# A hybrid decoder block on one core: which queue the third pair of experts' weights and the left-over rows come by, and when the place table is worked out

## The chip, the cores and the metric

The kernel runs on one core of a Trainium2 chip. The metric is the device time of one execution in microseconds (us), the median over several executions. A core has a matrix engine (TensorE, PE in the profile), two vector engines (VectorE, DVE, and ScalarE, ACT), GpSimd (POOL) and SyncE (SP). Transfers between the main memory and the on-chip memory are asked for by a queue of one of these engines. In this kernel SP's queue asks for nearly all weights, POOL's for everything that is gathered or scattered by row numbers.

## The reference

One decoder block over 512 tokens of width 1024: a state-space branch and a latent attention branch, a cross-attention to a memory, and a mixture of experts with 32 experts, of which each token takes two out of one group of eight. The change is in the mixture of experts alone:

```python
def hierarchical_moe(h, w_rg, b_rg, w_re, b_re, w_gate, w_up, w_down):
    ...
    g_sel = jnp.argmax(g_logits, axis=-1)
    ...
    top_v, top_i = lax.top_k(e_in, TOP_K)
    w_top = jax.nn.softmax(top_v, axis=-1) * g_w
    ...
    hg = jnp.einsum('td,edf->tef', t, w_gate)
    hu = jnp.einsum('td,edf->tef', t, w_up)
    act = jax.nn.silu(hg) * hu * combine[:, :, None]
    y = jnp.einsum('tef,efd->td', act, w_down)
    return y.reshape(b, s, d)
```

All data are float32. An expert's three matrices (gate and up 1024 x 256, down 256 x 1024) are 1024 KB each.

## The kernel before

The stages ahead of the experts and the routing, which finds every token's two experts, fill about the first 930 us of the profiled execution. The expert stage works on 16 *pairs* of experts, numbered 0 to 15 (`pr` in the code, `NP = 16`). Each expert has 64 places, so that a pair fills 128 rows, and places of which there are fewer tokens stay empty. (Tokens beyond 64 of an expert are handled after the loop; nothing there is touched.)

A pass of the loop over pairs does, for its pair `pr`:

- `gate_up(pr)`: 32 products of the gathered rows with the gate and up weights; after them it asks for the gate and up weights of pair `pr + 3` (`load_gate_up`, four transfers of 1024 KB). There are six slots for such weights (`gslots`), two to a pair, so three pairs are held.
- `hidden(pr)`: ACT and DVE form the hidden values (tile `ea`).
- `dispatch(pr + 1)`: eight transposes of the next pair's rows and their scaling on DVE into `XG`.
- `down_rows(pr - 1)`: the pair before's down product (`py`), and what becomes of it. It then asks for the down weights of pair `pr + 2` (`load_down`, two transfers; their tile is `dn`, or `dw` for every third pair).
- `turn(pr)`: two transposes of the hidden values for the down product of the next pass.
- `places(c)` in every second pass: the place table `PI[c]` for the two pairs of `c`, eight small products (`pinf`), one copy and 15 operations of DVE on 128 x 2 elements. It holds which token each place has, its weight and its scale. `onehots(c)` in the passes between builds the one-hot matrices for it.
- `fetch(pr + 3)`: POOL gathers that pair's rows (`GRt<-tD`) by the place table; an empty place's row number is out of bounds and skipped. There are two row buffers, `GR[0]` and `GR[1]`.

What becomes of a pair's down product differs. Pairs 0 to 6 (`NS = 7`): the 128 rows are scattered by POOL to a buffer in main memory (`yD<-YB`), at the place of their token. Pairs 7 to 15: the rows are added to the residual `h` at once, by products with one-hot matrices (`pcm`) and eight additions of DVE (`add_rows`). The rows that went to main memory are read back in 16 pieces of 256 KB (`left_rows`, tile `Yt<-yD`, two buffers), two at a time, the first two at the end of pass 7; in each of the passes 8 to 15, `add_left(2)` adds the two pieces that were asked for one pass earlier (DVE, `h<-h,Yt`) and then asks for the next two. Before, POOL's queue asks for them. These passes from 8 on are called *late* in the code.

Every engine and every queue takes its instructions in the order in which this stage's code gives them (`tc.manual_schedule()`). A transfer into a slot waits until the last reader of the slot is done. Besides, the transfers of SP and ACT use eight completion semaphores in turn, and one that is issued waits until the transfer that used its semaphore before has landed, eight transfers earlier. So about eight are under way at most.

Before the loop, `first_rows(0)` and `first_rows(1)` find the token numbers of the first two pairs by a product of one-hot matrices with the token numbers (`ptk`) and gather their rows by these; an empty place asks for row 0. `keep_warm(n)` is n transposes of the identity (`pw`) that nothing reads.

Of the kernel before, what the change touches and what calls it, by code (L numbers as in the profile page):

```python
# [11 lines left out]
I32 = mybir.dt.int32  # L12
# [5 lines left out]
S, D, M = 512, 1024, 256  # L18
NT, KD = S // 128, D // 128
# [10 lines left out]
def block(tc, nc, I, out, dbg=None):  # L30
# [3 lines left out]
    V, A, G, T = nc.vector, nc.scalar, nc.gpsimd, nc.tensor  # L34
# [7 lines left out]
    def pA(name="pa"):  # L42
        return ps.tile([128, 512], F32, name=name, tag="A", bufs=4)
# [29 lines left out]
    def keep_warm(n, p=None):  # L73

        p = pB("pw") if p is None else p
        for _ in range(n):
            T.transpose(p[:, :128], ident, ident)
# [145 lines left out]
    ss = const([128, NT], name="ss")  # L223
# [36 lines left out]
    p = pA()  # L260
# [707 lines left out]
    def gslot(pr, s, shape, name):  # L968
        return sb.tile(shape, F32, name=name, tag=gslots[(2 * pr + s) % 6])

    def load_gate_up(pr, ss=(0, 1)):
        for s in ss:
            w = gslot(pr, s, [128, 2, KD, 256], "gu")
            for j, m in enumerate(("w_exp_gate", "w_exp_up")):
                nc.sync.dma_start(w[:, j], I[m][0, pr * 2 + s].rearrange("(p k) n -> p k n", p=128))
            WG.setdefault(pr, []).append(w)

    def load_down(pr):
        tag = dslots[pr % 3]
        if tag:  # L980
            w = sb.tile([128, 2, 2, D], F32, name="dn", tag=tag)
            w = [w[:, s] for s in range(2)]
        else:
            w = [sb.tile([128, 2, D], F32, name="dw", tag="wr", bufs=2) for _ in range(2)]
        for s in range(2):
            nc.sync.dma_start(w[s], I["w_exp_down"][0, pr * 2 + s].rearrange("(p k) n -> p k n", p=128))
        WD[pr] = w


# [115 lines left out]
    def onehots(c):  # L1105

        for t in range(NT):
            o = OHs[c == 1][:, t]
            V.tensor_scalar(o, iot1[:, :256], slc[:, c - 1, 0, t:t + 1], None, op0=OP.is_equal)
            stt(o, iot1[:, :256], slc[:, c - 1, 1, t:t + 1], f(o), OP.is_equal, OP.add)  # L1110
# [8 lines left out]

    chain = ExitStack()  # L1120
    chain.enter_context(tc.manual_schedule())
    load_gate_up(2)
    load_down(2)
    for t in range(0, NT, 2):
        q = slice(t, t + 2)
        vn = sb.tile([128, 2], F32, name="vn", tag="rsv", bufs=4)
# [100 lines left out]
    def gather(pr, ix, **k):  # L1227
        G.indirect_dma_start(out=GR[pr % 2], out_offset=None, in_=tD, in_offset=bass.IndirectOffsetOnAxis(ap=ix, axis=0), **k)  # L1228

    def first_rows(j):  # L1230

        p = pB("ptk")
        ix = ov[:, 300 + j:301 + j].bitcast(I32)
        for t in range(NT):
            T.matmul(p[:, :2], OHs[0][:, t, j * 128:(j + 1) * 128], tok2[:, t], start=t == 0, stop=t == NT - 1)
        V.tensor_scalar(ix, p[:, :1], -1.0, 0.0, op0=OP.add, op1=OP.max)  # L1236
        gather(j, ix)

    def dispatch(pr):

# [7 lines left out]

    def places(c):

        p = pA("pinf")
        for j in range(2):
            for t in range(NT):
                T.matmul(p[:, j * 8:j * 8 + 8], OHs[c == 1][:, t, j * 128:(j + 1) * 128], info[:, t],
                         start=t == 0, stop=t == NT - 1)
        pi = PI[c] = ov[:, 216 + c % 3 * 26:242 + c % 3 * 26]
        V.tensor_copy(pi[:, :16], p[:, :16])
        col = lambda i: pi[:, :16].rearrange("p (j x) -> p x j", x=8)[:, i]
        ix, sx = (ov[:, o + c % 3 * 2:o + 2 + c % 3 * 2].bitcast(I32) for o in (300, 306))
        u, wa, w, hr, r = (pi[:, 16 + 2 * i:18 + 2 * i] for i in range(5))  # L1260
        V.tensor_scalar(u, col(0), 0.0, 4096.0, op0=OP.is_equal, op1=OP.mult)
        V.tensor_add(u, u, col(0))
        V.tensor_scalar(ix, u, -1.0, None, op0=OP.add)
        V.tensor_add(r, col(6), col(7))
        V.tensor_scalar(hr, r, 0.5, None, op0=OP.mult)
        V.tensor_sub(w, col(5), hcol)
        V.tensor_scalar(w, w, 4.0 * c, None, op0=OP.is_equal)
        stt(u, w, -float(S), u, OP.mult, OP.add)
        V.tensor_scalar(sx, u, S - 1.0, None, op0=OP.add)
        V.tensor_add(wa, col(1), col(2))  # L1270
        V.tensor_mul(w, w, wa)
        V.tensor_add(wa, col(3), col(4))
        V.tensor_add(w, w, wa)
        V.tensor_mul(r, r, r)
        V.tensor_mul(w, w, r)

    def fetch(pr):

        gather(pr, ov[:, 300 + pr // 2 % 3 * 2 + pr % 2:301 + pr // 2 % 3 * 2 + pr % 2].bitcast(I32),
               bounds_check=S - 1, oob_is_err=False)  # L1280
# [86 lines left out]
    first_rows(0)  # L1367
    first_onehots(1)
    first_rows(1)
    gfin = fo = None  # L1370
    wcol = lambda pr: PI[pr // 2][:, 20 + pr % 2:21 + pr % 2]
    hcol_ = lambda pr: PI[pr // 2][:, 22 + pr % 2:23 + pr % 2]
# [19 lines left out]
    def add_rows(pr, after=None):  # L1392
        combine(oTs.pop(pr), 128, after)
# [3 lines left out]
    def left_rows(n):  # L1397

        for i in range(ny[0], min(ny[0] + n, 16)):
            s, t, c = i // 8, i // 2 % 4, i % 2  # L1400
            G.dma_start(Yt[0][:, c], yD[s * S + t * 128:s * S + (t + 1) * 128, c * 512:(c + 1) * 512])
            ny[0] += 1

    def add_left(n):
# [4 lines left out]
            ny[1] += 1  # L1409
        left_rows(n)  # L1410

    keep_warm(6)
    dispatch(0)
    keep_warm(8)
    for pr in range(NP):
        p = gate_up(pr)
        if pr == 0:
            weights()
            onehots(1)
            dispatch(1)  # L1420
            places(1)
            fetch(2)
            fetch(3)
            places(0)
        HG[pr] = hidden(p, 128, "ea", hcol_(pr))
        if pr == 0:
            onehots(2)
            continue
        if pr == 1:
            turn(0)  # L1430
        late = pr > NS
        if late:
            down_rows(pr - 1)
        if pr + 1 < NP:
            dispatch(pr + 1)
        c = pr // 2 + 2
        if pr % 2 and c < NP // 2:
            places(c)
        elif c < NP // 2 and not late:
            onehots(c)  # L1440
        if pr + 3 < NP:
            fetch(pr + 3)
        if not late:
            down_rows(pr - 1)
        turn(pr)
        if pr == 2:
            overflow()
        if late:
            add_rows(pr - 1)
            add_left(2)  # L1450
            if pr % 2 == 0 and c < NP // 2:
                onehots(c)
        if pr == NS:
            Yt.append(sb.tile([128, 2, 512], F32, name="Yt", tag="WL0"))
            left_rows(2)
            W2.append([sb.tile([128, 512], F32R, name=f"Wx{i}", tag=t) for i, t in enumerate(("acT", "selP"))])
            W2.append([x[:, i * 512:(i + 1) * 512] for x in [sb.tile([128, 1024], F32R, name="Wy", tag="WL2")] for i in range(2)])
        if pr == NP - 2:
            fo = gslot(NP - 3, 0, [128, NT, D], "fo")
            gfin = gslot(NP - 3, 1, [128, D], "gfin")  # L1460
            row_bcast(gfin, I["norm_final"], D)
# [104 lines left out]
```

## Time and profile before

| | before |
|---|---|
| device time, median of 3 runs | 1220.15 us (1219.07 to 1221.02) |
| profiled execution: device time | 1216.74 us |
| profiled execution: span, first to last instruction | 1215.0 us |
| PE busy in the span | 1165.5 us (96%) |
| DVE / ACT / POOL busy | 732.1 / 498.0 / 95.2 us |
| moved by DMA in the span | 209.22 MB, mean 172 GB/s |

The profiled execution is 3.4 us shorter than the median of the runs, and 1.74 us of it lie outside the span. The page cuts the span in 40 slices of 30.4 us: in the last ten or so the DMA engines are busy nine tenths and more, at 416 to 421 GB/s. PE's busy time counts matmuls whose ends are modelled, so it is no measure of its speed.

### The profile page before, as it was taken

To read this page: it belongs to the slowest core of one execution; us is meant where nothing else is said; L and a number is where in the kernel's file an instruction comes from. 1 tells how busy PE (TensorE), PEld (TensorE's weight loads), DVE (VectorE), ACT (ScalarE), POOL (GpSimd) and SP (SyncE) were. 2 spreads that over 40 slices of the span, in tenths; PEclk is the share of its full clock that TensorE was granted. 3 is DMA by queue.
4 is the path that set the end of the run, shared out by engine and by line. 5 is a ranking of instruction groups with operands and counts; after the bars stand their busy time and mean duration, and the time that the engine had idled before them with its cause. 6 is when DMAs were issued, how large, how long until landed. Compare 5 with 4: busy or idle time off the path is not lost. (4 is left out here: it accounts for less than half of the span.)

```text
span 1215.0 us, 15732 instructions
## 1 busy us (share of the span) xinstructions
PE 1165.5 (96%) x5930; PEld 846.5 (70%) x5930; DVE 732.1 (60%) x1490; ACT 498.0 (41%) x941; POOL 95.2 (8%) x118
## 2 busy tenths in 40 slices
PE   8999999999999999999999999999997999999992
PEld 7786777777888888887776888988886433434441
DVE  4387788778872334646776745744525744467654
ACT  5434856767443123447775424533421011101112
POOL 0101112111000000101110000000000011111001
PEclk9999999999999999999999999999998899999996
DMA  3532424432323234320225373562817699999961
GB/s 114 160 113 63 144 67 137 122 115 62 97 94 104 70 104 123 98 60 22 55 83 178 105 242 104 174 214 70 339 42 312 248 417 421 416 417 417 417 279 70
DMA packets 103755, 209.22 MB, mean 172 GB/s; under 512 B 13343, under 2 KB 71484, under 8 KB 91390
## 3 DMA queue, kind: packets, MB, share of 16 engines
q1 hardware_dynamic: 96782, 193.11, 44.1%
q0 software_dynamic: 6320, 12.99, 3.2%
q10 hardware_dynamic: 576, 2.10, 0.4%
q8 instruction: 47, 0.77, 0.3%
q14 instruction: 30, 0.25, 0.1%
HBM read 199.33 MB, written 12.12 MB: 174 GB/s over the span
## 5 line engine op out<-in xcount | busy, mean ns | idle before, releaser
L150 DVE TENSOR_TENSOR WLt<-wr,WHt 128x1024 fp32r<-128x1024 f32 x124 | 153.4, 1239 | 176.4 <-ACT WHt L149 99.0
L149 ACT ACTIVATE WHt<-wr 128x1024 fp32r<-128x1024 f32 x125 | 132.2, 1059 | 267.9 <-PE pa L126 158.9
L126 PE MATMUL pa<-uh,WHt 128*128 128x512 f32 x488 | 128.0, 399 | 2.4 <-ACT WHt L149 2.4
L126 PE MATMUL pa<-ul,WHt 128*128 128x512 f32 x488 | 126.2, 397 | 0.0
L126 PE MATMUL pa<-uh,WLt 128*128 128x512 f32 x488 | 125.1, 394 | 0.0
L1296 PE MATMUL pgu<-gu,GRt 128*64 128x512 f32 x512 | 116.1, 598 | 0.9 <-DMA gu<-in_w_exp_up_dram 0.9
L126 PEld LDWEIGHTS pa<-uh,WHt 128*128 128x128 f32 x488 | 89.8, 188 | 23.1 <-ACT WHt L149 2.8
L126 PEld LDWEIGHTS pa<-ul,WHt 128*128 128x128 f32 x488 | 91.3, 190 | 19.2 <-issue 0.7
L126 PEld LDWEIGHTS pa<-uh,WLt 128*128 128x128 f32 x488 | 90.8, 188 | 19.6 <-issue 1.2
L1296 PEld LDWEIGHTS pgu<-gu,GRt 128*64 128x64 f32 x512 | 36.2, 138 | 70.6 <-issue 67.9
L1285 ACT ACTIVATE ea<-pgu,ov 128x256 f32<-128x256 f32 x16 | 7.6, 473 | 146.8 <-PE pgu L1296 133.9
L55 DVE SCALAR_TENSOR_TENSOR ea<-ea,pgu 128x256 f32<-128x256 f32 x16 | 6.7, 421 | 79.4 <-ACT ea L1285 79.4
L711 DVE TENSOR_REDUCE sm<-psc 128x1 f32<-128x512 f32 (+2 forms) x64 | 30.4, 489 | 23.5 <-PE psc L709 20.3
L1339 DVE TENSOR_TENSOR h<-h,pcm 128x512 f32<-128x512 f32 x72 | 43.8, 679 | 0.0
L1316 PE MATMUL py<-dn,aT 128*64 128x512 f32 x176 | 42.5, 617 | 0.0
L712 ACT ACTIVATE Pq<-psc,sm 128x512 f32<-128x512 f32 (+2 forms) x64 | 33.2, 528 | 10.6 <-DVE sm L711 10.2
L1228 POOL DMA_INDIRECT GRt<-tD,ov x16 | 16.5, 1030 | 260.8 <-DVE ov L1236 142.6
L55 DVE SCALAR_TENSOR_TENSOR y<-pa,cols,y 128x509 f32<-128x509 f32 (+2 forms) x48 | 34.7, 744 | 1.6 <-ACT y L383 1.4
L126 PE MATMUL pa<-yl,WHt 128*128 128x512 f32 x128 | 32.8, 396 | 0.0
L126 PE MATMUL pa<-yh,WLt 128*128 128x512 f32 x128 | 32.3, 394 | 0.0
L126 PE MATMUL pa<-yh,WHt 128*128 128x512 f32 x128 | 32.2, 393 | 0.0
L459 ACT ACTIVATE dc<-S6t,ac 128x128 f32<-128x128 f32 x96 | 30.4, 388 | 0.8 <-POOL y L476 0.8
(513 smaller groups left out, 2263.1 us busy)
## 6 DMA issues: line engine op xcount, KB each, us to landing
gu<-in_w_exp_gate_dram SPq DMA_DIRECT2D x32, 1024.0 KB, 19.8
gu<-in_w_exp_up_dram SPq DMA_DIRECT2D x32, 1024.0 KB, 21.7
wr<-in_w_in_dram SPq DMA_DIRECT2D x26, 1024.0 KB, 5.5
dn<-in_w_exp_down_dram SPq DMA_DIRECT2D x22, 1024.0 KB, 22.2
dw<-in_w_exp_down_dram SPq DMA_DIRECT2D x10, 1024.0 KB, 21.2
wr<-in_w_ssd_out_dram SPq DMA_DIRECT2D x8, 1024.0 KB, 5.0
wr<-in_w_xkv_dram SPq DMA_DIRECT2D x8, 1024.0 KB, 5.0
S6t<-ac_d SPq DMA_DIRECT2D x24, 256.0 KB, 4.2
```

The source lines that it names most:

```text
L55: V.scalar_tensor_tensor(o, a, s, b, op0=op0, op1=op1, **k)
L126: T.matmul(o, a(k)[x], b(k)[y], start=first and n == 0, stop=last and n == 3 * nk - 1)
L149: A.activation(h, raw, AF.Copy)
L150: lo.tensor_tensor(l, raw, f(h), op=OP.subtract)
L459: A.activation(dc[:, cs], R[:, cs], AF.Relu, scale=-1.0, bias=ac[:, c * 32 + h:c * 32 + h + 1])
L711: V.reduce_max(mx, dst, axis=AX.X, negate=True)
L712: A.activation(P[:, ROFF[qc]:ROFF[qc] + n], dst, AF.Exp, bias=mx, accum_out=sm[:, 1, s, qc:qc + 1])
L1228: G.indirect_dma_start(out=GR[pr % 2], out_offset=None, in_=tD, in_offset=bass.IndirectOffsetOnAxis(ap=ix, axis=0), **k)
L1285: A.activation(a[:, :256], p[:n, :256], AF.Tanh, scale=hr)
L1296: T.matmul(p[s * 64:(s + 1) * 64].rearrange("p (j n) -> p j n", j=2), XG[:, k, s * 64:(s + 1) * 64], gu[s][:, :, k], start=k == 0, stop=k ...
L1316: T.matmul(p[s * 64:(s + 1) * 64], aT[:, k, s * 64:(s + 1) * 64], dn[s][:, k, hf * 512:(hf + 1) * 512], start=k == 0, stop=k == 1)
L1339: V.tensor_add(h[:, t, hs], h[:, t, hs], p)
```

## The change

It has five parts.

1. The loads of pair 2, six transfers, all stood on SP's queue ahead of everything in this stage. Now the four that fill the pair's second expert's gate and up slot and both down slots stand on POOL's queue: gate and up behind the gathers of pairs 0 and 1, down behind the gather of pair 2.
2. `first_rows` now serves pairs 2 and 3 as well, in place of `fetch(2)` and `fetch(3)`. `onehots(1)` moves ahead of the first `dispatch`, and the place tables 0 and 1 are made in that order.
3. The 6 and 8 transposes of `keep_warm` around the first `dispatch` become 14 ahead of it.
4. In the late passes, `places(c)` is split: its products and the copy stay where they were, its 15 small operations and the gather of pair `pr + 3` follow the eight additions of `add_rows`.
5. The pieces `Yt` are asked for by SP's queue and no longer by POOL's.

```diff
-    def load_gate_up(pr, ss=(0, 1)):
+    def load_gate_up(pr, ss=(0, 1), q=nc.sync):
...
-                nc.sync.dma_start(w[:, j], I[m][0, pr * 2 + s].rearrange("(p k) n -> p k n", p=128))
+                q.dma_start(w[:, j], I[m][0, pr * 2 + s].rearrange("(p k) n -> p k n", p=128))
...
-    load_gate_up(2)
-    load_down(2)
+    load_gate_up(2, (0,))
...
-    def first_rows(j):
+    def first_rows(pr):
 
         p = pB("ptk")
-        ix = ov[:, 300 + j:301 + j].bitcast(I32)
+        ix = ov[:, 300 + pr:301 + pr].bitcast(I32)
+        j = pr % 2
         for t in range(NT):
-            T.matmul(p[:, :2], OHs[0][:, t, j * 128:(j + 1) * 128], tok2[:, t], start=t == 0, stop=t == NT - 1)
+            T.matmul(p[:, :2], OHs[pr // 2][:, t, j * 128:(j + 1) * 128], tok2[:, t], start=t == 0, stop=t == NT - 1)
         V.tensor_scalar(ix, p[:, :1], -1.0, 0.0, op0=OP.add, op1=OP.max)
-        gather(j, ix)
+        gather(pr, ix)
...
     first_rows(1)
+    load_gate_up(2, (1,), G)
+    onehots(1)
...
-            G.dma_start(Yt[0][:, c], yD[s * S + t * 128:s * S + (t + 1) * 128, c * 512:(c + 1) * 512])
+            nc.sync.dma_start(Yt[0][:, c], yD[s * S + t * 128:s * S + (t + 1) * 128, c * 512:(c + 1) * 512])
...
-    keep_warm(6)
+    keep_warm(14)
     dispatch(0)
-    keep_warm(8)
+    first_rows(2)
+    load_down(2, G)
     for pr in range(NP):
         p = gate_up(pr)
         if pr == 0:
             weights()
-            onehots(1)
             dispatch(1)
-            places(1)
-            fetch(2)
-            fetch(3)
-            places(0)
+            first_rows(3)
+            run(places(0))
+            run(places(1))
...
-        if pr % 2 and c < NP // 2:
-            places(c)
-        elif c < NP // 2 and not late:
-            onehots(c)
-        if pr + 3 < NP:
-            fetch(pr + 3)
-        if not late:
+        places_c = places(c) if pr % 2 and c < NP // 2 else iter(())
+        if late:
+            next(places_c, None)
+        else:
+            run(places_c)
+            if pr + 3 < NP:
+                fetch(pr + 3)
+            if pr % 2 == 0:
+                onehots(c)
             down_rows(pr - 1)
...
         if late:
             add_rows(pr - 1)
+            run(places_c)
+            if pr + 3 < NP:
+                fetch(pr + 3)
             add_left(2)
```

Three places of the instruction order show it. The first is SP's queue at the end of the routing, where the loads of pair 2 and then those of pair 3 stand (a `gu` row is one gate or up matrix, `-` is before, `+` is now):

```order
 L975 DMA gu<-in_w_exp_gate_dram 128x2048
 L975 DMA gu<-in_w_exp_up_dram 128x2048
-L986 DMA dw<-in_w_exp_down_dram 128x2048 x2
-L975 DMA gu<-in_w_exp_gate_dram 128x2048
-L975 DMA gu<-in_w_exp_up_dram 128x2048
 L975 DMA gu<-in_w_exp_gate_dram 128x2048
 L975 DMA gu<-in_w_exp_up_dram 128x2048
```

Four transfers have left the queue; the next ones on it are those of pair 3.

The second is POOL at the start of the stage, before (`GRt` is a gather, `yD` a scatter):

```order
L998 IOTA MI 128x512
L1015 IOTA MI 128x4
L1228 DMA GRt<-tD,ov 128x1024 x5
L1387 DMA yD<-YB,ov 1024x1024
L1228 DMA GRt<-tD,ov 128x1024
```

and now:

```order
L1227 DMA GRt<-tD,ov 128x1024 x2
L975 DMA gu<-in_w_exp_gate_dram 128x2048
L975 DMA gu<-in_w_exp_up_dram 128x2048
L1227 DMA GRt<-tD,ov 128x1024
L986 DMA dw<-in_w_exp_down_dram 128x2048 x2
L1227 DMA GRt<-tD,ov 128x1024 x2
L1396 DMA yD<-YB,ov 1024x1024
```

The four transfers stand between the gathers of pairs 1, 2 and 3.

The third is SP's queue around the end of pass 7, where the first two pieces are asked for; the loads ahead are the down weights of pair 9, those behind the gate and up weights of pair 11:

```order
 L975 DMA gu<-in_w_exp_up_dram 128x2048
 L986 DMA dn<-in_w_exp_down_dram 128x2048 x2
+L1410 DMA Yt<-yD 128x512 x2
 L975 DMA gu<-in_w_exp_gate_dram 128x2048
 L975 DMA gu<-in_w_exp_up_dram 128x2048
```

The same two rows come in once per pass from here on, always behind the pass's two down loads and ahead of the next pass's four gate and up loads; POOL has no such row any more.

## Rows read from the trace of the kernel before

**Rows 1.** Stretches: us, busy (count) of PE, PEld, DVE, ACT, POOL; clock, DMA share, GB/s.

```profile
934.00:942.00 8.00, 3.24 (x16) 2.87 (x17) 1.02 (x4) 0.00 (x0) 1.97 (x2) 0.59 0.81 338
942.00:953.00 11.00, 11.00 (x53) 5.42 (x52) 7.87 (x33) 0.42 (x2) 0.00 (x0) 0.84 0.01 1
...
969.00:1049.00 80.00, 79.82 (x398) 30.98 (x396) 33.83 (x124) 14.38 (x27) 13.50 (x15) 1.00 1.02 418
1065.00:1145.00 80.00, 75.43 (x352) 33.29 (x354) 53.47 (x122) 9.39 (x17) 9.68 (x14) 1.00 1.02 417
```

**Rows 2.** What PE waited for from 925 us on: us, times, longest.

```profile
PE pxg L1245 <- DMA GRt<-tD,ov: 5.6, 2, 3.8
...
PE pcm L1337 <- DVE h L1339: 3.8, 2, 1.9
...
PE pgu L1296 <- DMA gu<-in_w_exp_up_dram: 0.9, 2, 0.7
```

**Rows 3.** What SP's queue waited for from 1000 to 1160 us.

```profile
SPq L975 <- DMA dn<-in_w_exp_down_dram: 25.9, 10, 3.0
...
SPq L975 <- PE pgu L1296: 6.0, 1, 6.0
```

**Rows 4.** DMA issues from 1000 to 1160 us: count, KB each, median us to landing.

```profile
gu<-in_w_exp_gate_dram SPq DMA_DIRECT2D x18, 1024.0 KB, 23.2
...
Yt<-yD POOLq DMA_DIRECT2D x14, 256.0 KB, 7.6
...
GRt<-tD,ov POOLq DMA_INDIRECT x9, 8.4
```

**Rows 5.** SP's queue in order of time: start, us, instructions merged.

```profile
1062.01 3.94 SPq L986 DMA_DIRECT2D dn<-in_w_exp_down_dram  x2
1069.12 0.33 SPq L975 DMA_DIRECT2D gu<-in_w_exp_gate_dram  x1
...
1088.45 0.33 SPq L975 DMA_DIRECT2D gu<-in_w_exp_up_dram  x1
...
1136.17 0.33 SPq L975 DMA_DIRECT2D gu<-in_w_exp_gate_dram  x1
...
1148.26 2.81 SPq L986 DMA_DIRECT2D dw<-in_w_exp_down_dram  x2
```

**Rows 6.** DVE in order of time, passes 8, 9 and 13; idle time in brackets.

```profile
1065.52 1.28 DVE L1408 TENSOR_TENSOR h<-h,Yt 128x512 f32<-128x512 f32 x2
...
1073.39 0.42 DVE L55 SCALAR_TENSOR_TENSOR ea<-ea,pgu 128x256 f32<-128x256 f32 x1 [3.35 <-ACT ea L1285]
...
1079.04 0.17 DVE L1261 TENSOR_SCALAR ov<-ov 128x2 f32<-128x2 f32 x1
...
1081.32 0.16 DVE L1275 TENSOR_TENSOR ov<-ov 128x2 f32<-128x2 f32 x1
...
1154.12 1.28 DVE L1408 TENSOR_TENSOR h<-h,Yt 128x512 f32<-128x512 f32 x2
```

**Rows 7.** PE in order of time: start of the stage, then passes 14 and 15.

```profile
935.44 1.54 PE L77 MATMUL pw<-ident 128*128 128x128 f32 x6
940.77 1.97 PE L1245 MATMUL pxg<-ident,GRt 128*128 128x128 f32 x8 [3.79 <-DMA GRt<-tD,ov]
...
944.38 7.68 PE L1296 MATMUL pgu<-gu,GRt 128*64 128x512 f32 x32
951.99 1.16 PE L1245 MATMUL pxg<-ident,GRt 128*128 128x128 f32 x8
...
965.87 5.35 PE L1316 MATMUL py<-dn,aT 128*64 128x512 f32 x16
...
979.63 3.65 PE L1316 MATMUL py<-dn,aT 128*64 128x512 f32 x16
...
1152.53 7.09 PE L1296 MATMUL pgu<-gu,GRt 128*64 128x512 f32 x32
...
1168.87 7.09 PE L1296 MATMUL pgu<-gu,GRt 128*64 128x512 f32 x32
```

More of the change, by code (lines that the diff above doesn't have):

```diff
@@ L974, in load_gate_up, with load_down @@
             for j, m in enumerate(("w_exp_gate", "w_exp_up")):
-                nc.sync.dma_start(w[:, j], I[m][0, pr * 2 + s].rearrange("(p k) n -> p k n", p=128))
+                q.dma_start(w[:, j], I[m][0, pr * 2 + s].rearrange("(p k) n -> p k n", p=128))
             WG.setdefault(pr, []).append(w)
-    def load_down(pr):
+    def load_down(pr, q=nc.sync):
         tag = dslots[pr % 3]
@@ L985, in load_down @@
         for s in range(2):
-            nc.sync.dma_start(w[s], I["w_exp_down"][0, pr * 2 + s].rearrange("(p k) n -> p k n", p=128))
+            q.dma_start(w[s], I["w_exp_down"][0, pr * 2 + s].rearrange("(p k) n -> p k n", p=128))
         WD[pr] = w
@@ L1257, in places @@
         V.tensor_copy(pi[:, :16], p[:, :16])
+        yield
         col = lambda i: pi[:, :16].rearrange("p (j x) -> p x j", x=8)[:, i]
@@ L1275, in places, with run @@
         V.tensor_mul(w, w, r)
+        yield
+    def run(it):
+        for _ in it:
+            pass
     def fetch(pr):
```

## The prediction

> **What bounds the kernel now.** I read the busy time by stretch first. From 969 to 1145 us the DMA engines are at a share of 1.02 and 417 to 418 GB/s: there is no room for more bytes per second [rows 1]. PE's column is nearly full in the same stretch, so I asked next what PE waits for: from 925 us on it waits 5.6 us for gathers (in two places, at the start), 3.8 us for DVE's additions to `h` (two waits of 1.9) and only 0.9 us for weights [rows 2]. PE and the loads run neck and neck. SP's queue tells which leads: from 1000 us on its issues wait for earlier loads to land (25.9 us in this row alone), and for a gate-and-up product of PE just once [rows 3]. So the weight stream sets the pace from about pass 6 on and PE follows close behind. How close: SP's second `dw` of 1148.26 + 2.81 is issued at 1150.7, when the transfer eight places earlier, the last gate or up load of pair 14, has landed [rows 5]; PE begins with that pair at 1152.5 [rows 7], 1.8 us later.
>
> One pair is worth (1136.17 - 1069.12) / 4 = 16.8 us of this stream, between the first gate loads of pairs 11 and 15 [rows 5].
>
> **Parts 1 to 3, the start.** PE's gains first. The first gather shares the engines with pair 2's loads, and PE waits 3.8 us for it [rows 7]. Without four of the loads it may land up to 3.8 us earlier or no earlier; I take 1, since its issue and setting up stay. From 934 to 942 us the granted clock averages 0.59, a mix of 1.2 and 2.4 GHz, after PE had done little but short bursts; the first eight transposes take 1.97 us against 1.16 at the full clock, and the first gate-and-up 7.68 against 7.09 [rows 1, 7]. Fourteen transposes at the six's 0.26 us fill 3.6 us from 935.4, to 939.0, so PE is busy nearly until the gather lands; I count both differences, 0.8 and 0.6 (0 if the clock stays low). Of the eight transposes that stood behind the first dispatch, 0.8 us lay on the path. That is 3.2 us at the end of pass 0, less 0.6 for the four products of `first_rows(3)`, plus the second gather wait of 5.6 - 3.8 = 1.8 [rows 2], and plus 1.7 if pass 1's down product runs at 3.65 like the next one and not at 5.35 [rows 7]: some 6 us for PE by pass 2.
>
> Since the loads set the pace later, only what the stream gains counts. From 942 to 953 us the DMA share is 0.01 [rows 1]: pair 2 has landed and pair 3's slots come free when pass 0 ends, at 952.1 [rows 7]. In the change the four moved loads (4.19 MB) and one gather (0.52 MB) use that hole: at 418 GB/s they take 11.3 us from about 939.7, with 0.6 us between them to about 951.6, and pair 3's loads, asked for at about 948.9, follow without a break. Before, they moved from about 953.2 (an estimate: 1.1 us after the asking). The stream is 1.6 us ahead (0 if POOL's queue leaves gaps, 3 if the first load follows sooner). `gate_up(2)` needs the moved slot only at about 965 us; even the 23.2 us of a load in a full queue [rows 4] would bring it by 961. Gathers by token number move all 128 rows where skipped ones moved fewer, up to 0.52 MB or 1.3 us more; one of the two now lies in the hole, so I call it even.
>
> **Part 4, the place table.** The 15 small operations (1079.04 to 1081.48) stand in pass 9 ahead of the additions that free PE's banks [rows 6]; behind them PE loses 1.9 us in passes 9 and 11 each [rows 2]. Both waits go. The gather that now follows takes 8.4 us [rows 4] and is needed two passes later, so it stays hidden behind 30 us of work.
>
> **Part 5, the left-over rows.** The row first: in one and the same stretch a 1024 KB load on SP's queue lands 23.2 us after its issue, a piece `Yt` on POOL's queue 7.6 us, a gather there 8.4 [rows 4]. SP's loads stand in line behind one another; POOL's transfers pass that line. The Trainium skill (DMA: Bandwidth & Descriptors, "Queues, rings and completion order") says just this: each DMA engine takes the descriptors of one queue's ring in order and goes round between the rings. Its section "Issuing engines are not separate DMA queues" pulls the other way: which engine issues only saves issue time. By that part of the Trainium skill part 5 would cost nothing, and the sum would be that of the first rival below; by the row it costs what follows. I go by the row.
>
> The first two pieces now stand behind pair 9's down loads, whose second is issued at 1062.01 + 3.94 - 0.33 = 1065.6, and has landed when the eighth transfer behind it is issued, at 1088.4 [rows 5]. In the change the two pieces follow it (2 x 256 KB, 1.3 us); ahead of it are missing the four pieces that POOL had already brought by then (1.05 MB, 2.5 us), and the stream is 1.6 earlier: 1088.4 - 1.6 - 2.5 + 1.3 = 1085.6. DVE needs them for the addition at the end of pass 8, which now begins at 1065.5 [rows 6]. It can end at 1085.6 + 0.7 = 1086.3, 19.5 us later than now. DVE works in order: behind the addition stand pair 9's hidden values (at 1073.4 now [rows 6]), its turn on PE, the next scaling and additions. PE gets through `gate_up(9)`, the down product and the transposes and then stands still for some 15 us.
>
> From there it repeats. SP's next pieces wait for that addition, since they use the same two buffers, and pair 12's loads wait behind them. But in front are all six loads of the next pair, 6.3 MB, so the engines stay full; the pieces land one pair later, and the addition of pass 9 ends 16.8 us after that of pass 8. The DVE has 53.5 us of work in 80 [rows 1], PE takes 1168.87 - 1152.53 = 16.3 us a pass without the waits [rows 7], so both keep that pace and neither catches up. Part 4's 3.8 us are swallowed here. Five passes on, pass 13's addition ends at 1086.3 + 5 x 16.8 = 1170.1 (5 x 16.76 = 83.8). Before, it ended at 1154.12 + 1.28 = 1155.4, and 1215.0 - 1155.4 = 59.6 us remained. The pieces of the last two passes have only two loads ahead of them and come in time; of the 59.6 us PE will have done about 1 more of `gate_up(14)` during the wait (between 0 and 4).
>
> **Sum.** The span becomes 1170.1 + 59.6 - 1.0 = 1228.7 us, 13.7 more than 1215.0. The profiled execution was 1216.74, 3.4 under the median of 1220.15, so I add to the median: **1234 us**. Bounds: with a stream 3 us ahead and 3 us more done in the waits, 1229.5; with no gain of the stream, and PE at the low clock after its 15 us of standing still (the down product's 1.7 us [rows 7], and some of that again in later passes, together 5), 1241. That is the likeliest case's own range.
>
> **Rivals.**
> - *The pieces come in time* (faster). Place: the addition at the end of pass 8. If a small transfer on SP's queue lands as soon as on POOL's, parts 1 to 4 remain: the stream's 1.6 us, and the 1.8 that PE trails behind it, since PE's own gains (6 and 3.8) are larger. 1220.15 - 3.4 = 1216.8. By the sum, the change breaks even when the first pieces land 13.7 us earlier than I say, at about 1071.9; that asks that they pass some 6 MB of loads. For it: they are small. Against it: 23.2 against 7.6 us [rows 4]. This is also where the Trainium skill's sentence on issuing engines leads; rows 4 do not bear it out. Chance 0.11.
> - *The queue runs dry too* (slower still). If SP, held at the pieces, issues the next pair so late that the engines stand idle about 2 us in each of five passes, 10 us are added: 1244. Against it: eight transfers are exactly one pass's, and all six loads are ahead of the wait. Chance 0.08.
> - *The start brings nothing.* If POOL issues 1024 KB transfers slowly, or the gathers of pairs 2 and 3 stand behind them too long, the stream's 1.6 us are lost and pass 2 waits up to 2: 1236 to 1238. No row of before has a load of that size on this queue. Chance 0.07.
>
> **How the numbers follow.** My forecast has 0.74. What a measurement of this kernel can tell from no change is 0.2%, 2.4 us. Faster is the first rival, with 0.10 of its 0.11 clear of that bound; the other 0.01 and 0.03 of the forecast's (first pieces that land near 1072) are within 0.2%; slower is the rest, 0.86. Nothing lies between the first rival and my own range, so the range reaches upwards: 1226 to 1244 holds nearly all of the forecast's 0.74, the third rival and half of the second.
>
> **What would show it.** Right: `Yt` on SP with a median to landing near 20 us; DVE idle for about 20 us in pass 8, ended by a piece, and some 5 us in the passes after; PE idle about 15 us between 1070 and 1090; pass 13's additions near 1170; the DMA share at 1.0 all the while; the hole at 942 filled; no wait of PE for DVE's additions in passes 9 and 11. Wrong: pieces that land within 8 us, or an addition of pass 8 that ends before 1072. If the span between the additions of passes 9 and 13 is not 67 us, the stream is not what paces them.

## The result, and the profile after

| | before | changed |
|---|---|---|
| device time, median of 6 runs each, side by side | 1219.34 us (1215.32 to 1221.02) | 1229.13 us (1226.1 to 1230.34) |
| ratio to before, 95% interval | | 1.008 (1.0062 to 1.0099) |
| profiled execution: device time, span | 1216.74, 1215.0 us | 1229.52, 1227.7 us |

The changed kernel is slower by 0.8%, some 9.8 us. The stretches of the changed kernel, with the columns of [rows 1], show where to look:

```profile
942.00:953.00 11.00, 11.00 (x55) 6.17 (x51) 5.04 (x28) 0.42 (x2) 2.21 (x4) 0.84 0.98 385
953.00:969.00 16.00, 10.69 (x53) 5.74 (x54) 8.47 (x43) 1.33 (x3) 0.85 (x1) 0.91 1.00 397
...
1065.00:1145.00 80.00, 66.05 (x297) 33.30 (x298) 47.14 (x111) 8.32 (x15) 2.97 (x3) 0.89 1.02 417
1101.00:1200.00 99.00, 98.87 (x455) 42.62 (x456) 67.90 (x143) 13.30 (x24) 3.96 (x4) 1.00 0.79 320
```

The hole at 942 us is filled: a DMA share of 0.98 where it was 0.01 [rows 1]. Then PE has gaps in 953 to 969, which the prediction had not seen. From 1065 on the loads are as full as before, 1.02 and 417 GB/s, but PE is busy for 66.05 us of 80 and not for 75.43 [rows 1]. So the DMA engines moved as much as ever, and PE did less beside them. What PE lacks lies ahead of 1101 us: from there to 1200 it is busy for 98.87 us of 99. The waits from 925 us on, answering to [rows 2], name the cause of both (engine, tile and line, what ended the wait; us, times, longest):

```profile
DVE h L1417 <- DMA Yt<-yD: 33.2, 5, 20.2
...
PE pinf L1255 <- DVE OH L55: 13.7, 5, 12.3
...
DVE ov L1265 <- DMA GRt<-tD,ov: 6.6, 1, 6.6
...
PE pat L1314 <- DVE ea L1295: 5.1, 1, 5.1
...
PE pxg L1245 <- DMA GRt<-tD,ov: 1.6, 1, 1.6
```

`h L1417` is the addition of the pieces: DVE waits 33.2 us for them in five waits, the longest 20.2. PE then waits for DVE: `OH` are the one-hot matrices that DVE builds right behind the addition of pass 8, and PE's products for the place table in pass 9 (`pinf`) need them; 12.3 us at once. PE's waits for additions to `h`, 3.8 us in [rows 2], are gone. The row numbers' write (`ov L1265`) waits 6.6 us for a gather; that is new as well.

The additions of the pieces in order of time, passes 8 to 13, which answer to the first and last lines of [rows 6] (idle time in brackets):

```profile
1088.60 1.35 DVE L1417 TENSOR_TENSOR h<-h,Yt 128x512 f32<-128x512 f32 x2 [20.23 <-DMA Yt<-yD]
1104.80 1.35 DVE L1417 TENSOR_TENSOR h<-h,Yt 128x512 f32<-128x512 f32 x2
1122.50 1.34 DVE L1417 TENSOR_TENSOR h<-h,Yt 128x512 f32<-128x512 f32 x2 [3.46 <-DMA Yt<-yD]
1138.69 1.35 DVE L1417 TENSOR_TENSOR h<-h,Yt 128x512 f32<-128x512 f32 x2 [0.72 <-DMA Yt<-yD]
1156.46 1.34 DVE L1417 TENSOR_TENSOR h<-h,Yt 128x512 f32<-128x512 f32 x2 [4.46 <-DMA Yt<-yD]
1172.66 1.33 DVE L1417 TENSOR_TENSOR h<-h,Yt 128x512 f32<-128x512 f32 x2 [4.32 <-DMA Yt<-yD]
```

From the end of pass 8's (1089.95) to that of pass 13's (1173.99) it is 84.0 us, five times 16.8. SP's queue where the first pieces stand, answering to [rows 5]:

```profile
1064.40 2.77 SPq L986 DMA_DIRECT2D dn<-in_w_exp_down_dram  x2
1070.52 2.76 SPq L1410 DMA_DIRECT2D Yt<-yD  x2
1075.47 0.33 SPq L975 DMA_DIRECT2D gu<-in_w_exp_gate_dram  x1
```

The first piece is asked for at 1070.5, and DVE gets the two at 1088.6, 18 us later. Over 1000 to 1160 us the issues give the same, beside the gathers that POOL's queue still asks for [rows 4]:

```profile
Yt<-yD SPq DMA_DIRECT2D x12, 256.0 KB, 16.2
GRt<-tD,ov POOLq DMA_INDIRECT x9, 8.5
```

### The profile page after: what moved, and what is told of

It is laid out like the page before. It is cut to its first block, busy times and chain, and to the rows that moved or that the text cites. A ratio compares the mean times of both kernels' runs of the same rounds, so it can differ in the third digit from the quotient of the medians.

```text
span 1227.7 us, 15737 instructions
## 1 busy us (share of the span) xinstructions
PE 1169.2 (95%) x5938; PEld 858.0 (70%) x5938; DVE 731.9 (60%) x1492; ACT 498.3 (41%) x941; POOL 88.6 (7%) x106
## 5 line engine op out<-in xcount | busy, mean ns | idle before, releaser
L1303 PEld LDWEIGHTS pgu<-gu,GRt 128*64 128x64 f32 x512 | 41.1, 138 | 64.1 <-issue 58.0
L712 ACT ACTIVATE Pq<-psc,sm 128x512 f32<-128x512 f32 (+2 forms) x64 | 33.3, 529 | 10.6 <-DVE sm L711 10.2
## 6 DMA issues: line engine op xcount, KB each, us to landing
gu<-in_w_exp_gate_dram SPq DMA_DIRECT2D x31, 1024.0 KB, 16.2
dn<-in_w_exp_down_dram SPq DMA_DIRECT2D x22, 1024.0 KB, 16.2
```

Source lines behind the costliest of these rows:

```text
L712: A.activation(P[:, ROFF[qc]:ROFF[qc] + n], dst, AF.Exp, bias=mx, accum_out=sm[:, 1, s, qc:qc + 1])
L1303: T.matmul(p[s * 64:(s + 1) * 64].rearrange("p (j n) -> p j n", j=2), XG[:, k, s * 64:(s + 1) * 64], gu[s][:, :, k], start=k == 0, stop=k ...
```

## The experiments

The theories as they stood when the first runs were made:

- **A**: DVE, which works in order, waits in pass 8 for pieces that stand behind pair 9's down loads in SP's queue. This is the whole loss.
- **B** (rival): the loss lies at the start, in the wait of 6.6 us for the gather, and the loads never catch up.
- **C** (rival, from the second set on): pieces on SP's queue have a fixed price, by the queue's hold or DVE's waits, wherever they stand.

### Part 5 taken out, and part 5 alone

In the changed kernel, and the reverse of it in the kernel before (`e2_only_part5`):

```diff
-            nc.sync.dma_start(Yt[0][:, c], yD[...])
+            G.dma_start(Yt[0][:, c], yD[...])
```

> The changed kernel with part 5 undone alone: the pieces Yt are asked for by POOL's queue again. Theory A (DVE, which works in order, waits at the end of pass 8 for pieces that stand behind pair 9's down loads on SP's queue, and this wait is the whole loss): that wait of 20 us is gone, pieces land in 7 to 8 us, PE's idle 12.3 us at 1090 us is gone, and the time is that of before within 3 us, 1216 to 1222, since the stream stays some 2 us late from the wait of 6.6 us at the start. Theory B (the loss comes from the start: the row number's write waits for a gather, PE falls to half its clock, the loads fall behind and never catch up): the time stays at 1226 to 1230.

> The kernel before with part 5 alone: the pieces Yt are asked for by SP's queue. Theory A: the pieces land 15 to 20 us after the asking, the addition of pass 8 ends near 1087 us, and from there 16.8 us a pass: 1228 to 1235, 9 to 15 us over the kernel before. The rival that small transfers on SP's queue come as soon as on POOL's: 1217 to 1222, no difference. If theory B of the run before holds (the start is the loss), also no difference here.

Measured: 1215.94 us, ratio 0.9983 (0.9969 to 0.9997), with the pieces back on POOL's queue; 1233.35 us, ratio 1.0132 (1.0109 to 1.0155), with part 5 alone. So part 5 alone is the loss, and more: without it the change is a small gain. B falls: the wait at the start is still there in the first kernel (6.1 us), and the loss is not. Over 1000 to 1160 us of the first kernel:

```profile
gu<-in_w_exp_up_dram SPq DMA_DIRECT2D x18, 1024.0 KB, 23.2
...
Yt<-yD POOLq DMA_DIRECT2D x14, 256.0 KB, 8.1
```

The same pieces that take 16.2 us on SP's queue take 8.1 here, beside loads that take 23.2. In the second kernel the first addition again waits:

```profile
1086.66 1.35 DVE L1408 TENSOR_TENSOR h<-h,Yt 128x512 f32<-128x512 f32 x2 [20.29 <-DMA Yt<-yD]
```

### Own columns for the row numbers

`first_rows(2)` and `(3)` keep their row numbers in columns 302 and 303 of `ov`, from which POOL's gathers read them; `places(1)` writes the same two columns (`ix`, L1265). The edit gives `first_rows` columns of its own, in the changed kernel, and together with the pieces on POOL's queue (`e4_own_index_pool_pieces`):

```diff
-        ix = ov[:, 300 + pr:301 + pr].bitcast(I32)
+        ix = ov[:, 312 + pr:313 + pr].bitcast(I32)
```

> The changed kernel, with four columns of the table for the row numbers of first_rows that nothing else writes (312 to 315 in place of 300 to 303). Theory A: DVE's wait of 6.6 us at 962.7 us and PE's of 5.1 us at 965.9 us are gone, pass 2 begins some 4 to 6 us sooner, the loads run some 3 to 3.5 us earlier up to pair 9's down loads, and the first pieces land near 1084.5 in place of 1088. The time falls by 3 to 3.5 us against the changed kernel, to 1225 to 1226; it stays 4 to 9 us over the kernel before, because the wait for the pieces is still there. Theory B: 1217 to 1221, the whole loss is gone.

> The changed kernel with both: own columns for the row numbers, and the pieces asked for by POOL's queue. Parts 1 to 4 are left, without the wait at the start. Theory A: both losses gone, 2 to 4 us below the kernel before, 1215 to 1217.5: the loads are 1.6 us ahead and PE's 1.8 us of lag behind them go with the waits of passes 9 and 11. The rival that the start brings nothing: equal to the kernel before within 1.5 us.

Measured: 1226.17 us, ratio 1.0071 (1.0053 to 1.0089), and 1213.65 us, ratio 0.9965 (0.9952 to 0.9978). The second is 1.4 us below what was expected. The write now waits for nothing in either. In the first kernel:

```profile
955.90 0.17 DVE L1265 TENSOR_SCALAR ov<-ov 128x2 int32<-128x2 f32 x1
...
1084.31 1.35 DVE L1417 TENSOR_TENSOR h<-h,Yt 128x512 f32<-128x512 f32 x2 [18.45 <-DMA Yt<-yD]
1101.11 1.29 DVE L1417 TENSOR_TENSOR h<-h,Yt 128x512 f32<-128x512 f32 x2
...
1168.43 1.33 DVE L1417 TENSOR_TENSOR h<-h,Yt 128x512 f32<-128x512 f32 x2 [3.38 <-DMA Yt<-yD]
```

All additions come some 4 us sooner than in the changed kernel, and the profiled span is 1224.5 us in place of 1227.7. By the ratios to before (1.0080 and 1.0071) the gain is nearer to 1 us, and their intervals overlap; between the two kernels with the pieces on POOL's queue, timed side by side, it is 2.3 us (1215.94 to 1213.65). The wait of DVE in pass 8 stays, and so does most of the loss. The second kernel, parts 1 to 4 without the unforeseen wait, has the lowest ratio here of all that do the whole work, though its interval overlaps that of `f3` below.

### Where the first pieces stand, and when they are needed

First (`f1`, in `down_rows`) the pieces of pass 8 alone ahead of pair 9's two down loads; then (`f2`, in the loop and behind it) the first addition one pass later, in pass 9:

```diff
+        if pr == NS - 1:
+            Yt.append(...)
+            left_rows(2)
         if pr + 3 < NP:
             load_down(pr + 3)
...
         if pr == NS:
-            Yt.append(...)
-            left_rows(2)
```

```diff
-            add_left(2)
+            if pr > NS + 1:
+                add_left(2)
...
     down_rows(NP - 1)
+    add_left(2)
```

> The changed kernel with one shift: the first two pieces Yt are asked for on SP's queue ahead of pair 9's two down loads in place of behind them. Theory A in its graded form (what counts is how many bytes stand ahead of the first pieces; all later passes follow it at the stream's pace): two loads of 1024 KB less ahead, 2 x 2.5 = 5 us; the first pieces land near 1083 in place of 1088 us, the addition of pass 8 and all that follows comes 5 us sooner, and the time is 1222 to 1225. Rival C (the loss is a fixed price of pieces on SP's queue, by its issue waits or by DVE's waits in each pass): no difference, 1226 to 1230.

> The changed kernel, but pass 8 leaves the addition of its two pieces out, so that the first pieces, asked for at the same place on SP's queue, are needed one pass later, and the last two are added behind the loop. Theory A (lateness against the need is the whole loss): the pieces land near 1088 us as they did, the addition of pass 9 would come at 1085 without a wait, so DVE waits 3 to 5 us there in place of 20 in pass 8; then 16.8 us a pass. 1217 to 1221, 8 to 11 us under the changed kernel. Rival C (SP's queue held at the pieces, and the loads late behind it): the hold is the same from pass 9 on, so 1226 or more.

Measured: 1228.68 us, ratio 1.0082 (1.0065 to 1.0098), and 1230.18 us, ratio 1.0095 (1.0077 to 1.0113). Both expectations by A failed: neither edit gave anything back. The first kernel's additions in passes 8, 9, 10 and 13:

```profile
1082.17 1.35 DVE L1420 TENSOR_TENSOR h<-h,Yt 128x512 f32<-128x512 f32 x2 [14.12 <-DMA Yt<-yD]
1104.06 1.33 DVE L1420 TENSOR_TENSOR h<-h,Yt 128x512 f32<-128x512 f32 x2 [5.51 <-DMA Yt<-yD]
1121.02 1.35 DVE L1420 TENSOR_TENSOR h<-h,Yt 128x512 f32<-128x512 f32 x2 [7.05 <-DMA Yt<-yD]
...
1171.30 1.32 DVE L1420 TENSOR_TENSOR h<-h,Yt 128x512 f32<-128x512 f32 x2 [2.10 <-DMA Yt<-yD]
```

The first pieces come 6.4 us sooner, as A says. But the second pieces stand where they stood, behind pair 10's down loads; DVE waits 5.5 and 7.1 us in the next two passes, and by pass 13 all but 1.4 us of it is gone. PE is held in passes 9 and 11, and it begins with pair 12 no earlier than in the changed kernel (first here, then there):

```profile
1134.83 7.09 PE L1303 MATMUL pgu<-gu,GRt 128*64 128x512 f32 x32
```

```profile
1133.96 7.09 PE L1303 MATMUL pgu<-gu,GRt 128*64 128x512 f32 x32
```

The second kernel, passes 9 and 10:

```profile
1087.09 1.36 DVE L1417 TENSOR_TENSOR h<-h,Yt 128x512 f32<-128x512 f32 x2 [0.55 <-DMA Yt<-yD]
1119.69 1.35 DVE L1417 TENSOR_TENSOR h<-h,Yt 128x512 f32<-128x512 f32 x2 [19.16 <-DMA Yt<-yD]
```

Pass 9 has its pieces almost without a wait, 0.55 us where 3 to 5 were expected. The next two, asked for after that addition because there are two buffers, stand behind pair 11's down loads, and the wait of 19 us comes in pass 10. It moved and did not shrink. So a single late first piece was the wrong picture, and either C is right or a new theory:

- **D**: in every pass the addition is tied to the loads that stand ahead of its pieces. Asked for at the end of pass p - 1, the pieces of pass p stand behind pair p + 1's down loads, which PE needs only in pass p + 2. DVE, and PE with it, are pushed back once by the lead that the queue of loads has over them, and stay there.

### The same queue, asked for two passes ahead

Four buffers of this size don't fit where the two lie, so three kernels leave out half of the pieces' columns (what they compute is not the whole block): on POOL's queue (`h0`), on SP's as in the change (`h1`), and on SP's with two sets of two buffers, each set asked for two passes ahead of its addition (`h2`). The last differs from `h1` by:

```diff
-            nc.sync.dma_start(Yt[0][:, 0, c], ...
+            nc.sync.dma_start(Yt[0][:, i // 2 % 2, c], ...
...
-            add_left(2)
+            if pr > NS + 1:
+                add_left(2)
+            else:
+                left_rows(2)
...
     down_rows(NP - 1)
+    add_left(2)
```

> Leaves out half of the left-over rows' columns: each of the 16 pieces is 128 x 256 (128 KB) in place of 128 x 512, so that four buffers fit where two did. Otherwise the changed kernel with the pieces on POOL's queue: the floor for the two runs beside it. All theories: the same kernel with whole pieces was 2.1 us under the kernel before; 2.1 MB less in all at 417 GB/s is 5 us, of which PE, 1.8 us behind the loads, follows at most 4. 1211 to 1216.

> The changed kernel with the same half pieces, left on SP's queue and asked for one pass ahead, as in the changed kernel. Theory D (in every pass the addition can't be earlier than the landing of the down loads that stand ahead of its pieces; what the engines lose is the lead that the queue of loads has over PE, once): the first pieces still land behind pair 9's down loads, near 1088 us, DVE waits 20 us, and at 16.2 to 16.3 us a pass the addition of pass 13 ends near 1170. 1223 to 1227. If the size of the pieces made the loss, half pieces would cost half: 1217 to 1220.

> As the run beside it, with the pieces asked for two passes ahead: SP's queue asks for two at the ends of passes 7 and 8 each (four buffers), the additions run from pass 9, the last two behind the loop. Bytes, sizes and queue are the same as in the run beside it; only each piece's place in the queue against its use moves by one pair. Theory D: the addition of pass 9 waits for pair 9's down loads, 2 to 3 us, and those of the later passes wait for nothing; 2 to 3 us over the half pieces on POOL's queue, 1214 to 1219. Rival C (a price of SP's queue itself, whatever the place): 1223 or more, like the run beside it.

| half pieces | median | ratio to before (95%) |
|---|---|---|
| `h0`, POOL's queue | 1212.06 us | 0.9953 (0.9937 to 0.997) |
| `h1`, SP's queue, one pass ahead | 1228.6 us | 1.0085 (1.0065 to 1.0104) |
| `h2`, SP's queue, two passes ahead | 1212.33 us | 0.9948 (0.9928 to 0.9968) |

`h2` has no loss at all; C falls and D stands, for half pieces; whole ones were not tried two passes ahead. D's size was off: it had expected 1214 to 1219, 2 to 3 us over `h0`, and `h2` is 0.3 over it. The pieces of `h1` and of `h2`, by issue, spend as long on the way as each other (KB each, median us to landing; first `h1`, then `h2`):

```profile
Yt<-yD SPq DMA_DIRECT2D x12, 128.0 KB, 15.7
```

```profile
Yt<-yD SPq DMA_DIRECT2D x13, 128.0 KB, 16.3
```

And DVE in `h2`, passes 9 and 10:

```profile
1086.58 0.77 DVE L1417 TENSOR_TENSOR h<-h,Yt 128x256 f32<-128x256 f32 x2
1103.66 0.76 DVE L1417 TENSOR_TENSOR h<-h,Yt 128x256 f32<-128x256 f32 x2 [3.07 <-DMA Yt<-yD]
```

DVE waits four times, at most 3.1 us, and it is its own slack: PE is busy for 79.92 us of the 80 from 1065 on. `h1` missed its expectation from above, by 1.6 us at the median: half pieces cost at least as much (16.5 us over `h0`) as whole ones (11.8 us, by the ratios 1.0080 and 0.9983). What is paid for is the place in the line against the need, not the bytes.

### Part 4 alone, and the start alone

`f3` is the kernel before with part 4 alone; `f4` is the best kernel (`e4`) with part 4 undone. This is the edit of `f4`:

```diff
-        if late:
-            next(places_c, None)
-        else:
-            run(places_c)
-            ...
+        run(places_c)
+        if pr + 3 < NP:
+            fetch(pr + 3)
...
             add_rows(pr - 1)
-            run(places_c)
-            if pr + 3 < NP:
-                fetch(pr + 3)
```

> The kernel before with part 4 alone: in the late passes the 15 small operations and the gather follow the eight additions. Theory A (the loads set the pace, PE is 1.8 us behind them): PE's two waits of 1.9 us go, of the 3.8 us at most the 1.8 of PE's lag reach the end; 0 to 1.8 us under the kernel before, 1216.4 to 1218.5. Rival (PE sets the pace): 3.8 us under it, 1214.5.

> The kernel with own columns for the row numbers and the pieces on POOL's queue, and with part 4 undone: parts 1 to 3 alone without the wait on the gather. Theory A: the loads are 1.6 us ahead (0 to 3), and the time is that much under the kernel before, 1215 to 1218; PE's waits of 1.9 us are there again in passes 9 and 11. With part 4 it was 1213.65, so 1 to 2 us of that gain should be part 4's. Rival (the start brings it all): 1213 to 1214.

Measured: 1215.29 us, ratio 0.9977 (0.9965 to 0.9989), 2.8 us under before (1.3 to 4.3); and 1216.17 us, ratio 0.9979 (0.9965 to 0.9993), 2.6 under (0.9 to 4.3). The interval of `f3` holds both the 1.8 of theory A and the 3.8 of its rival, so the time alone decides nothing. Its profile says more, though it is one execution against one. SP's down loads of pair 9, asked for in pass 7, before part 4 changes anything, and the first gate load of pair 11:

```profile
1061.05 3.94 SPq L986 DMA_DIRECT2D dn<-in_w_exp_down_dram  x2
1067.85 0.33 SPq L975 DMA_DIRECT2D gu<-in_w_exp_gate_dram  x1
```

They stand at 1062.01 and 1069.12 in before [rows 5], so this execution is 1.0 to 1.3 us ahead already, by chance. The span is 1212.0 us, 3.0 shorter than before's, which leaves 1.7 to 2.0 for part 4: as much as PE's lag of 1.8. In `f4` PE's two waits are there again:

```profile
PE pcm L1344 <- DVE h L1346: 3.8, 2, 1.9
```

### Transposes in PE's wait

> The changed kernel with 80 transposes of the identity, which nothing reads, in pass 9 ahead of the place table's products, where PE stands still for 12.3 us and its clock then falls to half from 1082 to 1099 us. Theory D: DVE's waits for pieces and the loads set the pace there, so the clock may stay full and the time doesn't change: 1227 to 1230, as the changed kernel, at most 1 us either way. Rival (the slow clock after the wait is part of the loss): 2 to 4 us less, 1224 to 1226.

```diff
-    def places(c):
+    def places(c, warm=0):
...
         p = pA("pinf")
+        keep_warm(warm, p)
...
-        places_c = places(c) if pr % 2 and c < NP // 2 else iter(())
+        places_c = places(c, 80 if pr == NS + 2 else 0) if pr % 2 and c < NP // 2 else iter(())
```

Measured: 1228.01 us, ratio 1.008 (1.0064 to 1.0096), the changed kernel's own. First the stretch of the wait in the changed kernel; then, here, the transposes and the stretch behind them (columns as in the first fence):

```profile
1082.00:1099.00 17.00, 6.52 (x18) 4.96 (x19) 10.02 (x21) 0.38 (x1) 0.00 (x0) 0.50 1.02 419
```

```profile
1076.67 8.90 PE L77 MATMUL pinf<-ident 128*128 128x128 f32 x80
```

```profile
1088.00:1098.00 10.00, 8.08 (x22) 6.17 (x23) 9.32 (x20) 0.38 (x1) 0.00 (x0) 0.50 1.01 419
```

PE's clock is at 1.2 GHz through all of it in the changed kernel. Here it is at 2.4 GHz (granted 1.00) while the transposes run. They end at 1085.6, PE then stands for 2.7 us, and from 1088 to 1098 us, where its real work is, the clock is at 1.2 GHz again. So the run hardly tests the rival: that the time stayed says little of what the low clock costs. The changed kernel's own rows bound it. DVE's additions of pass 9, at the low clock, and of pass 10, at the full one, and PE's next `gate_up` behind each:

```profile
1096.87 1.41 DVE L1346 TENSOR_TENSOR h<-h,pcm 128x512 f32<-128x512 f32 x2
...
1114.18 4.86 DVE L1346 TENSOR_TENSOR h<-h,pcm 128x512 f32<-128x512 f32 x8
```

```profile
1101.03 7.09 PE L1303 MATMUL pgu<-gu,GRt 128*64 128x512 f32 x32
1117.37 7.09 PE L1303 MATMUL pgu<-gu,GRt 128*64 128x512 f32 x32
```

Up to 1096.87 DVE has worked without a gap since the pieces came at 1088.60, so PE's clock cost nothing there. From the first addition to `gate_up` it is 4.2 us in pass 9 and 3.2 in pass 10. By this estimate the low clock cost about 1 us of the 9.8.

## Why the prediction was right, and where its sizes were off

The direction was right, and for the reason given; the time was 4.9 us too high, inside the stated range and just under the 1229.5 at which the likeliest case was to end. By its own steps:

| step | predicted | changed kernel | with own columns (`e3`) |
|---|---|---|---|
| addition of pass 8 ends | 1086.3 | 1089.95 | 1085.7 |
| DVE's wait there | about 20 | 20.2 | 18.5 |
| PE stands still | about 15 | 12.3 | 10.7 |
| from pass 9's addition to pass 13's | 67 | 67.8 | 67.4 |
| addition of pass 13 ends | 1170.1 | 1174.0 | 1169.8 |
| from there to the end | 58.6 | 53.7 | 54.7 |
| span | 1228.7 | 1227.7 | 1224.5 |

- **The bound.** The DMA engines are full, a share of 1.02 at 417 GB/s in both kernels, and the additions of the pieces follow the loads, five passes at 16.8 us to the tenth. PE does not: once it goes on, behind pass 8's wait, nothing holds it again (see the remainder). PE's 1.8 us behind the loads in the kernel before agree with what `f3` gained.
- **The start: a step that failed.** "PE some 6 us earlier by pass 2" and "the stream 1.6 us ahead" left out that `first_rows(2)` and `(3)` put their row numbers in columns that the place table writes. The write waits until the gather that reads them has landed:

```profile
962.74 0.17 DVE L1265 TENSOR_SCALAR ov<-ov 128x2 int32<-128x2 f32 x1 [6.63 <-DMA GRt<-tD,ov]
```

  Behind it on DVE stand pair 0's hidden values, and PE's next instruction waits for them. This is the changed kernel from pass 0 to pass 2, where [rows 7] showed before's:

```profile
940.21 1.16 PE L1245 MATMUL pxg<-ident,GRt 128*128 128x128 f32 x8 [1.56 <-DMA GRt<-tD,ov]
...
941.70 8.85 PE L1303 MATMUL pgu<-gu,GRt 128*64 128x512 f32 x32
...
965.86 0.58 PE L1314 MATMUL pat<-ident,ea 128*128 128x128 f32 x2 [5.07 <-DVE ea L1295]
...
975.31 1.08 PE L1303 MATMUL pgu<-gu,GRt 128*64 128x512 f32 x4
```

  Pass 2 begins at 975.3, later than the end of before's down product at 971.2 [rows 7], not earlier. Without that wait PE's gain is there: in `f4` it begins with pair 2 at 965.2, 6.3 us ahead of before's 971.5. The 1.6 us of the loads are not shown apart from chance. In `e4` the first gate load of pair 11 is asked for at 1067.69, 1.4 us ahead of before's 1069.12 [rows 5], but in `f3`, whose start is before's, it is 1.3 ahead as well. By the times, the start alone (`f4`) is worth 2.6 us, between 0.9 and 4.3. Of the clock's two terms one came in the change: its first eight transposes took 1.16 us, for 1.97 before. The first `gate_up` took 8.85 us, not 7.09, the granted clock in 942 to 953 us being 0.84. The first gather's wait fell from 3.8 to 1.6 us [rows 2], 2.2 for the 1 I took.
- **Part 4.** Both waits of 1.9 us went, and the gather behind the additions delayed nothing; worth 1.7 to 2.0 us by the profile of `f3`, 1.3 to 4.3 by its times. Swallowed in the change, as predicted.
- **Part 5.** The line behind the down loads, DVE's wait and the pace after it came as worked out, late by the 3.7 to 3.9 us that the start lost. PE stood for 12.3 us and not 15, and the pieces' median to landing was 16.2 us and not near 20. `h2` shows what the price hangs on: the place in the line against the pass that needs the piece, not SP's queue as such. The prediction's sentence that "in front are all six loads of the next pair" says so already, and the expectations of `f1` and `f2`, written later, forgot it. The Trainium skill (DMA: Bandwidth & Descriptors, "Issuing engines are not separate DMA queues") would have had the queue cost nothing but issue time. `e1` and `e2` show some 12 and 16 us (from their ratios). `h2` shows the condition: with its pieces needed one pass later the queue cost nothing (0.9948 against 0.9953 on POOL's).
- **The remainder: mis-sized.** Of the last passes PE had done not 1 us more in its waits but some 4.4: it begins with pair 14 at 1166.67, 7.3 us ahead of the end of pass 13's addition, against 2.9 before (1152.53 and 1155.4, [rows 6, 7]).

```profile
1166.67 7.09 PE L1303 MATMUL pgu<-gu,GRt 128*64 128x512 f32 x32
1183.00 7.09 PE L1303 MATMUL pgu<-gu,GRt 128*64 128x512 f32 x32
```

  The step that failed here is "both keep that pace and neither catches up". DVE waits for pieces in passes 10, 12 and 13, but PE waits for nothing from 1101 us on: from pair 10 (1101.03) to pair 15 (1183.00) it takes 16.4 us a pass, its own pace. It was held back once, and its own work then sets the end of the span. So the 3.5 to 4.5 us that DVE waits in these later passes cost no time. Another 1.4 us lie behind PE's last product (21.2 us to the end of the span, 22.6 before); why is open. This 4.9 and the start's loss nearly cancel in the span, which is 1.0 off: that is luck.
- **The median.** The 3.4 us by which the profiled execution of before lay under its median were carried over. The changed kernel's profiled execution (1229.52) lies at its median (1229.13). This is most of the 4.9 us, and chance: one execution stood for the kernel.

The rivals: the pieces did not come in time, the queue did not run dry (a share of 1.02), and the start did bring nothing in the change itself, though not for the reason given there: POOL issues a 1024 KB load in 0.6 us, and it lands after 9 us.

## What to carry to other kernels

In this kernel a transfer on a queue that runs ahead comes when what stands ahead of it has come: asked for two loads sooner, the first pieces came 6.4 us sooner (`f1`). Before moving one there, compare its place in the line with the first use of what stands in front. Here those loads were needed later than the piece; DVE, and PE behind it, were held back once, by 12 to 16 us of time, with pieces of 256 KB and of 128 KB alike. Ask earlier (with more buffers) or use a queue without a line. A wait that is seen later in the trace need not cost anything: look whether the engine that ends last still waits behind it. And where row numbers of a gather share a table with anything, the table's next writer can wait for the gather to land, 6.6 us here: give them their own columns. A version with both, `e4`, beats the kernel before by 0.35% (0.22 to 0.48) and the changed one by 1.1%.

## What was not expected of the hardware

- A write to the columns that hold an indirect gather's row numbers waited 6.63 us, to 962.74, for the gather's landing; POOL had issued it by 953.9. Whether the gather still reads them so late no run shows; the program waits for it.
- Halving the pieces took nothing off the loss: 16.5 us with 128 KB, 11.8 with 256 KB, each against the same pieces on POOL's queue.
- A load of 1024 KB asked for by POOL's queue landed 8.2 to 10.2 us after its issue at the start, where few others were under way, in the changed kernel:

```profile
dw<-in_w_exp_down_dram POOLq DMA_DIRECT2D x2, 1024.0 KB, 9.2
...
gu<-in_w_exp_gate_dram POOLq DMA_DIRECT2D x1, 1024.0 KB, 8.3
gu<-in_w_exp_up_dram POOLq DMA_DIRECT2D x1, 1024.0 KB, 10.2
```
